# A two-layer decoder trunk on one core: the distance between weight splits kept between units of weights instead of between their parts

## The chip, the cores and the metric

The kernel runs on one core of one Trainium2 chip. The metric is the device time of one execution in microseconds (us). The core's engines are named as the profile names them: PE (TensorE, matmuls; PEld is its weight load), DVE (VectorE), ACT (ScalarE), POOL (GpSimd) and SP (SyncE, which issues most DMAs here). Each engine works through its own list of instructions in the written order and waits at an instruction until what that one needs is done.

## What is computed

A trunk of two layers over 512 tokens and 16 prepended meta tokens, in float32, width 1024. Each layer is half a SwiGLU feed-forward step, a token mixer, and another half feed-forward step, each with an RMSNorm on its input and its output. The mixer of the first layer is gated linear attention. The second layer, which the change touches, attends locally: 16 query heads, 4 shared key/value heads, blocks of 128 queries that see the block before, their own block up to themselves, and the 16 meta keys:

```python
q = (hn @ w_q).reshape(B, L, N_KV_HEADS, GROUP, HEAD_DIM)
q = (apply_partial_rope(q, cos, sin) * (HEAD_DIM ** -0.5)).transpose(0, 2, 3, 1, 4)
s = jnp.einsum('bkgnqd,bknsd->bkgnqs', q_blk, k_band)
p = sink_softmax(s, mask, sink_b[None, :, :, None, None, None])
o_real = jnp.einsum('bkgnqs,bknsd->bkgnqd', p.astype(v.dtype), v_band)
return o @ w_out
```

## The kernel before

**Weights.** Every weight matrix is cut into units in the order of use. A unit is mostly 128 x 1024 numbers and is read in two parts of 128 x 512 into `raw` buffers, of which there are 11. A part is then split for PE into two rounded halves, whose sum is the float32 weight: ACT writes the high half (line 237), and DVE subtracts it from the raw part to give the low half (line 238). The split parts lie in 32 slots; `slot(i)` lets a unit's part wait until a slot is free. A product with a split weight takes three matmuls for each of the eight 128-wide blocks of the inner dimension, and blocks 0 to 3 use the unit's first part, 4 to 7 its second.

**What sets the order.** The program is written by generators (`Flow`, `Job`) that run against a clock of the writer's own. The clock goes forward with each matmul that is written and has nothing to do with the chip. A generator that yields a number is taken up again when the clock has gone that far. So the instructions of loading, splitting, softmax and output are written between the matmuls where the clock calls for them, and this order is fixed in the program. Each engine keeps it.

**Local attention (`swa`, from about 1345 to 1500 us of the profiled span).** Eight query units u of 128 columns hold two heads each, 64 rows apiece. The first four are made by `x_first`, the others by `x_units` one after the other (PE tile `x`, 128 x 512, bank of PSUM). Line 1170 to 1173 rotate a product into `q`: a shuffle on DVE, a multiplication on DVE which also frees the bank, and two operations on POOL. For each u, `soft` writes four blocks of scores: two matmuls `sc`, one for each head, on the upper and on the lower 64 rows of PE; then on DVE, for each of the two, a masked minimum that reads the bank (line 1285, two rows of the trace), on ACT the exponential (line 1292); then sum, reciprocal and division (lines 1294 to 1308; for the second head, POOL divides). `core` transposes the result (`pt` and `pp` on PE), copies it (line 1327 on ACT, line 1328 on DVE), and makes the output `o`, which line 408 and 409 split into `so`. Last come the output products `y`. PSUM has eight banks here, all from one pool; a matmul that begins a new tile waits until the bank's last reader is done.

Splits of query units 5 to 7 and of the output weights (`swa_out`) run in this stretch. There `gap[0]` is 2.2 in place of 0: it is the smallest distance, in the writer's clock, between two splits. `turn[0]` holds the time of the last one. Elsewhere in the program `gap[0]` is 0 and the changed lines do nothing.

Of the kernel before, what the change touches and what calls it, by code (L numbers as in the profile page):

```python
# [127 lines left out]
def trunk_kernel(ctx: ExitStack, tc, a, out):  # L128
    nc = tc.nc
    pe, act, dve, pool, sp = nc.tensor, nc.scalar, nc.vector, nc.gpsimd, nc.sync  # L130
    flow = Flow()
# [50 lines left out]
    gap, turn = [0.0], [0.0]  # L182
# [42 lines left out]
    def slot(i):  # L225

        while live[0] + sum(n for j, n in owed.items() if j < i) >= limit[0]:
            yield room[0]
        live[0] += 1
        owed[i] -= 1  # L230

    def raw_tile(name):
        return rp.tile([P, 512], F32, tag="raw", name=name)

    def split_part(i, raw, m):
        w = pair_tile(f"w{i}_{len(loaded[i])}")
        act.activation(w[:, 0, :m], raw[:, :m], AF.Copy)  # L237
        newest[0] = hold(dve.tensor_tensor(w[:, 1, :m], raw[:, :m], w[:, 0, :m].bitcast(F32), op=ALU.subtract))  # L238
        loaded[i].append(w)

    def split_unit(i, raws, x):
        yield 2.2
        if x is not None:
            yield x.built[1]
        for raw, m in raws:
            if gap[0]:
                turn[0] = max(turn[0] + gap[0], flow.clock)
                yield turn[0] - flow.clock
            yield from slot(i)
            bound[0] = x and x.low  # L250
            split_part(i, raw, m)
            bound[0] = None
# [40 lines left out]
    def load_unit():  # L293
        i = len(loaded)
        asked[0] += costs[i]
        owed[i] = costs[i]
        if isinstance(units[i], list):
            g, u = units[i]
            chains[0] += 1
            raws = [raw_tile(f"raw{i}_{k}") for k in range(5)]  # L300
            for k, src, c in ((0, g, 0), (3, u, 0), (4, g, 0), (2, u, 1), (1, g, 1)):
                sp.dma_start(raws[k], src[:, c * 512 : (c + 1) * 512])
                dma_end[0] = max(dma_end[0], flow.clock) + 512 * 1.5e-3
            names = ("11", "12", "22", "s1", "s2", "s3", "s4")
            loaded.append(({k: [] for k in names}, {k: Job(None) for k in names}))
            gen = split_pair(i, raws)
        else:
            n = units[i].shape[-1]
            raws = []
            for c in range(0, n, 512):  # L310
                m = min(512, n - c)
                raws.append((raw_tile(f"raw{i}_{c}"), m))
                sp.dma_start(raws[-1][0][:, :m], units[i][:, c : c + m])
            dma_end[0] = max(dma_end[0], flow.clock) + n * 1.5e-3
            loaded.append([])
            gen = split_unit(i, raws, behind_x[0])
        split_jobs.append(flow.spawn(gen, dma_end[0] - flow.clock))
# [1073 lines left out]
    raws = [[raw_tile(f"raw{i}_{c}") for c in (0, 512)] for i in range(2)]  # L1391
# [151 lines left out]
```

## Time and profile before

| | us |
|---|---|
| median of 3 runs (1861.32 to 1862.3) | 1862.29 |
| the profiled execution | 1861.54 |
| its span, first to last instruction | 1859.8 |
| PE busy in the span | 1843.0 |
| DVE busy | 1360.3 |
| ACT busy | 1006.5 |
| POOL busy | 314.9 |

The profile is of one execution. A row of its timeline gives the start in us from the span's start, the length of the group, the engine, the line, output tile and inputs, the shape, and how many instructions were put together; in brackets stands the idle time ahead of it and what ended it. Matmuls overlap, so the time that one costs PE is the distance to the start of the next row, not its length. A float32 matmul, such as a score, has two instructions in the trace, so x4 means two scores.

### The profile page before, as it was taken

What the parts mean: (1) busy time and instruction counts of PE and PEld (TensorE: products, weight loads), DVE (VectorE), ACT (ScalarE), POOL (GpSimd) and SP (SyncE); (2) the same over time, 40 slices, a digit from 0 to 9 for tenths busy, and PEclk for the clock granted to TensorE, in tenths of its full rate; (3) what the DMA queues carried; (4) which work ended last, traced back from release to release, by engine and by line L of the source; (5) the groups of instructions that cost most, each with busy time, mean ns of one, the idle gap of its engine ahead of it and who ended that gap; (6) DMA issues with size and microseconds to landing.
All of it is one profiled execution on the core that took longest, in us unless ns stands there. A gap on an engine that the chain in (4) does not pass through costs nothing.

```text
span 1859.8 us, 36852 instructions
## 1 busy us (share of the span) xinstructions
PE 1843.0 (99%) x14146; PEld 1758.7 (95%) x14146; DVE 1360.3 (73%) x2703; ACT 1006.5 (54%) x2191; POOL 314.9 (17%) x370
## 2 busy tenths in 40 slices
PE   8999999999999999999999999999999999999998
PEld 8999999999999999999999898989977898989897
DVE  7884758777585887584888785858799589858484
ACT  7662636564465575362665563536556566626363
POOL 2101011320002310101033001111353231010101
PEclk9999999999999999999999999999999999999999
DMA  5655656312113255565642456666311215565561
GB/s 199 154 151 137 155 147 161 125 58 80 57 47 114 69 147 159 131 156 136 169 159 58 104 154 154 150 154 169 127 58 47 80 43 137 156 146 161 142 177 47
DMA packets 132530, 231.32 MB, mean 124 GB/s; under 512 B 14848, under 2 KB 26624, under 8 KB 132352
## 3 DMA queue, kind: packets, MB, share of 16 engines
q1 hardware_dynamic: 111328, 191.07, 32.6%
q0 software_dynamic: 20736, 37.76, 13.0%
q8 instruction: 111, 1.82, 0.4%
q14 instruction: 67, 0.55, 0.1%
q10 hardware_dynamic: 288, 0.13, 0.0%
HBM read 226.80 MB, written 2.10 MB: 123 GB/s over the span
## 4 chain that ended last, share of the span: by engine, by line
PE 89%; DVE 7%; ACT 3%; issue 1%; DMA 0%; POOL 0%; DVEq 0%; SPq 0%; ACTq 0%
PE y L165 29%; PE a L165 22%; PE x L165 16%; PE c L165 10%; PE d L165 5%; PE o L165 1%; PE e L165 1%; PE yt L165 1%; PE po L165 1%; DVE w L238 1%; ACT w L237 1%; PE sc L165 1%; DVE H L473 1%; PE ps L165 0%; PE pt L177 0%
## 5 line engine op out<-in xcount | busy, mean ns | idle before, releaser
L270 POOL DMA_DIRECT2D raw<-in_w_in x144 | 126.0, 953 | 970.1 <-DMA raw<-in_w_in 316.6
L165 PE MATMUL y<-hidl0f,w 128*128 128x256 f32 (+1 forms) x2112 | 260.4, 285 | 0.0
L238 DVE TENSOR_TENSOR w<-raw,w 128x512 fp32r<-128x512 f32 x376 | 241.2, 669 | 25.4 <-ACT w L237 23.5
L165 PEld LDWEIGHTS y<-hidl0f,w 128*128 128x128 f32 x2112 | 258.6, 188 | 0.2
L264 ACT ACTIVATE w_s<-raw 128x512 fp32r<-128x512 f32 x288 | 177.7, 625 | 116.4 <-DVE raw L280 69.5
L265 DVE TENSOR_TENSOR w_s<-raw,w_s 128x512 fp32r<-128x512 f32 x288 | 195.2, 689 | 55.3 <-ACT w_s L264 53.4
L165 PE MATMUL y<-hidl1f,w 128*128 128x512 f32 (+1 forms) x1200 | 233.2, 354 | 0.0
L165 PEld LDWEIGHTS y<-hidl1f,w 128*128 128x128 f32 x1200 | 195.1, 188 | 32.9 <-DVE w L238 0.3
L237 ACT ACTIVATE w<-raw 128x512 fp32r<-128x512 f32 x376 | 206.7, 587 | 34.2 <-PE y L165 28.0
L265 DVE TENSOR_TENSOR w<-raw,w 128x512 fp32r<-128x512 f32 x216 | 145.6, 688 | 51.9 <-ACT w L264 51.0
L264 ACT ACTIVATE w<-raw 128x512 fp32r<-128x512 f32 x216 | 130.4, 620 | 43.1 <-PE y L165 37.6
L165 PE MATMUL x<-x_l0m,w 128*128 128x272 f32 (+1 forms) x1152 | 148.2, 287 | 0.0
L165 PEld LDWEIGHTS x<-x_l0m,w 128*128 128x128 f32 x1152 | 142.5, 188 | 1.2 <-issue 0.4
L601 DVE TENSOR_TENSOR Y<-y,Y 128x256 f32<-128x256 f32 (+2 forms) x160 | 75.5, 479 | 88.4 <-PE y L165 88.2
L165 PE MATMUL a<-zl0f_t,w_s 128*128 128x264 f32 x864 | 117.5, 285 | 0.0
L165 PE MATMUL a<-zl1f_t,w_s 128*128 128x256 f32 x864 | 114.5, 282 | 0.6 <-ACT c L892 0.4
L165 PEld LDWEIGHTS a<-zl0f_t,w_s 128*128 128x128 f32 x864 | 110.4, 188 | 0.0
L165 PEld LDWEIGHTS a<-zl1f_t,w_s 128*128 128x128 f32 x864 | 107.2, 188 | 1.7 <-ACT c L892 1.6
L403 POOL TENSOR_TENSOR acc_post<-acc_post,sq_post 128x256 f32<-128x256 f32 (+1 forms) x72 | 60.9, 847 | 263.5 <-ACT sq_post L402 260.7
L165 PE MATMUL x<-x_l0f,w 128*128 128x256 f32 (+1 forms) x768 | 97.7, 289 | 5.8 <-ACT w L237 5.6
L165 PEld LDWEIGHTS x<-x_l0f,w 128*128 128x128 f32 x768 | 96.0, 191 | 6.6 <-ACT w L237 5.6
L165 PE MATMUL x<-x_l1f,w 128*128 128x256 f32 (+1 forms) x576 | 92.2, 320 | 0.0
(394 smaller groups left out, 3371.3 us busy)
## 6 DMA issues: line engine op xcount, KB each, us to landing
raw<-in_w_in SPq DMA_DIRECT2D x424, 256.0 KB, 3.8
raw<-in_w_in POOLq DMA_DIRECT2D x144, 256.0 KB, 5.3
raw<-in_w_out SPq DMA_DIRECT2D x96, 256.0 KB, 3.5
raw<-in_w_last SPq DMA_DIRECT2D x48, 256.0 KB, 3.3
raw<-in_gla_in SPq DMA_DIRECT2D x48, 256.0 KB, 3.1
raw<-in_w_out SPq DMA_DIRECT2D x64, 128.0 KB, 3.0
raw<-in_gla_out SPq DMA_DIRECT2D x16, 256.0 KB, 2.7
raw<-in_w_q SPq DMA_DIRECT2D x16, 256.0 KB, 4.1
```

Of the source, the lines that this page charges most:

```text
L165: inst = pe.matmul(o, lhs, rhs, start=start, stop=stop, skip_group_check=onto)
L237: act.activation(w[:, 0, :m], raw[:, :m], AF.Copy)
L238: newest[0] = hold(dve.tensor_tensor(w[:, 1, :m], raw[:, :m], w[:, 0, :m].bitcast(F32), op=ALU.subtract))
L264: act.activation(w[:, 0, :512], src, AF.Copy)
L265: dve.tensor_tensor(w[:, 1, :512], src, w[:, 0, :512].bitcast(F32), op=ALU.subtract)
L270: pool.dma_start(dst, src, accum_op=ALU.add)
L403: pool.tensor_tensor(sums[0][:, :n], sums[0][:, :n], t[:, :n], op=ALU.add)
L473: dve.tensor_tensor(h, t, h, op=ALU.add)
L601: dve.tensor_tensor(y, p[:, :n], y, op=ALU.add)
```

## The change

Before, each of a unit's two parts takes the next turn, 2.2 of the writer's clock behind the one before. Two units that are waiting at the same time take turns alternately, so that their parts are written interleaved: the first part of unit 5, the first of unit 6, and so on. After, a unit takes one turn for both parts, 2 x 2.2 behind the turn before, and its second part is written right behind the first if a slot is free. No operation is added or removed; nothing about the work of an instruction changes.

```diff
-        for raw, m in raws:
-            if gap[0]:
-                turn[0] = max(turn[0] + gap[0], flow.clock)
+        for c, (raw, m) in enumerate(raws):
+            if gap[0] and c == 0:
+                turn[0] = max(turn[0] + gap[0] * len(raws), flow.clock)
                 yield turn[0] - flow.clock
             yield from slot(i)
```

Since the turns come otherwise, the matmuls between them come otherwise too. Three places are shown. In the names, `x_0_17190` or `x_0_17185` is the product of query unit 5, `w_0` and `w_1` are the first and second part of a unit's split weights, `sc_eb` is the score of head e in block b, and the last number counts buffers in the order of writing.

The first is on PE, at query unit 5, from its fourth block on; before:

```order
L165 MATMUL x_0_17190<-x_l1m_16674,w_0_17146 128x512 x3
L165 MATMUL x_0_17190<-x_l1m_16699,w_1_17187 128x512
L165 MATMUL sc_00_17213<-kz_12401,q_17037 128x144
L165 MATMUL sc_10_17215<-kz_12401,q_17037 128x144
L165 MATMUL sc_01_17230<-kz_12401,q_17037 128x272
L165 MATMUL x_0_17190<-x_l1m_16699,w_1_17187 128x512 x2
L165 MATMUL x_0_17190<-x_l1m_16719,w_1_17187 128x512 x3
L165 MATMUL x_0_17190<-x_l1m_16744,w_1_17187 128x512 x3
L165 MATMUL sc_11_17232<-kz_12401,q_17037 128x272
```

and after:

```order
L165 MATMUL x_0_17185<-x_l1m_16674,w_0_17146 128x512 x3
L165 MATMUL x_0_17185<-x_l1m_16699,w_1_17149 128x512 x3
L165 MATMUL x_0_17185<-x_l1m_16719,w_1_17149 128x512 x3
L165 MATMUL sc_00_17219<-kz_12401,q_17037 128x144
L165 MATMUL sc_10_17221<-kz_12401,q_17037 128x144
L165 MATMUL x_0_17185<-x_l1m_16744,w_1_17149 128x512 x3
L165 MATMUL x_0_17185<-x_l1m_16769,w_1_17149 128x512 x3
L165 MATMUL sc_01_17233<-kz_12401,q_17037 128x272
L165 MATMUL sc_11_17235<-kz_12401,q_17037 128x272
```

The scores of block 1 stood on the two sides of eight matmuls; now they are next to each other, and five more matmuls of the unit's second part stand ahead of the first score. On DVE, the second part's split `w_1_17187` stood 16 instructions behind that of the first, `w_0_17146`; now, as `w_1_17149`, it follows it directly.

The second is on DVE, at the product of query unit 6 (`x_0_17280`, after `x_0_17248`), which the rotation (lines 1170 and 1171) takes out of its bank; before:

```order
L1285 ISA s_0_17340,nm_17342<-sc_01_17367,away,nsink 128x272
L1285 ISA nm_17342 128x1
L1285 ISA s_1_17341,nm_17342<-sc_11_17369,away,nsink 128x272
L1285 ISA nm_17342 128x1
L238 TENSOR_TENSOR w_0_17373<-raw_0_17239,w_0_17373 128x512
L1170 STREAM_SHUFFLE sh_q_16_17384<-x_0_17280 128x512
L1171 TENSOR_TENSOR q_17383<-x_0_17280,csq 128x512
```

and after:

```order
L1170 STREAM_SHUFFLE sh_q_16_17376<-x_0_17248 128x512
L238 TENSOR_TENSOR w_0_17358<-raw_0_17175,w_0_17358 128x512
L238 TENSOR_TENSOR w_1_17361<-raw_512_17177,w_1_17361 128x512
L1171 TENSOR_TENSOR q_17375<-x_0_17248,csq 128x512
L1285 ISA s_0_17346,nm_17348<-sc_01_17387,away,nsink 128x272
L1285 ISA nm_17348 128x1
```

Two splits now stand between the two steps that empty the bank; the two minima of block 1, which stood ahead of these steps, come behind them.

The third is on DVE too, at the scores of the third query unit's last block (`sc_03` and `sc_13`) with the division of the second unit (lines 1305 and 1308) between them; before:

```order
L238 TENSOR_TENSOR w_1_17425<-raw_512_17174,w_1_17425 128x512
L1298 RECIPROCAL den_17260<-den_17260 128x8
L1285 ISA s_0_17340,nm_17342<-sc_03_17430,away,nsink 128x272
L1285 ISA nm_17342 128x1
L1305 TENSOR_TENSOR mt_17262<-Y,den_17260 128x16
L1305 TENSOR_TENSOR mt_17262<-Y,den_17260 128x48
L1308 TENSOR_TENSOR Y<-Y,den_17260 128x144
L1308 TENSOR_TENSOR Y<-Y,den_17260 128x816
L1305 TENSOR_TENSOR mt_17262<-Y,den_17260 128x16
L1305 TENSOR_TENSOR mt_17262<-Y,den_17260 128x48
L1285 ISA s_1_17341,nm_17342<-sc_13_17432,away,nsink 128x272
```

and after:

```order
L1298 RECIPROCAL den_17270<-den_17270 128x8
L238 TENSOR_TENSOR w_0_17431<-raw_0_17239,w_0_17431 128x512
L1305 TENSOR_TENSOR mt_17272<-Y,den_17270 128x16
L1305 TENSOR_TENSOR mt_17272<-Y,den_17270 128x48
L1308 TENSOR_TENSOR Y<-Y,den_17270 128x144
L1308 TENSOR_TENSOR Y<-Y,den_17270 128x816
L1305 TENSOR_TENSOR mt_17272<-Y,den_17270 128x16
L1305 TENSOR_TENSOR mt_17272<-Y,den_17270 128x48
L238 TENSOR_TENSOR w_1_17434<-raw_512_17241,w_1_17434 128x512
L1285 ISA s_1_17347,nm_17348<-sc_13_17441,away,nsink 128x272
```

The minimum of `sc_13`, whose bank PE's first `o` takes next, now has two splits ahead of it in this place where it had one.

The order differs only from query unit 5 to the last split of the output weights; behind that, each engine's list is as before. SP's list of loads has the same loads in the same order, and POOL's differs at one place, where a rotation and a division change places.

## The prediction

> **What bounds the kernel.** I read the page first: the busy times, then the chain that ended last.
>
> ```profile
> span 1859.8 us, 36852 instructions
> PE 1843.0 (99%) x14146; PEld 1758.7 (95%) x14146; DVE 1360.3 (73%) x2703; ACT 1006.5 (54%) x2191; POOL 314.9 (17%) x370
> ...
> PE 89%; DVE 7%; ACT 3%; issue 1%; DMA 0%; POOL 0%; DVEq 0%; SPq 0%; ACTq 0%
> ```
>
> PE is the bound, and DMA has no share of the chain. The change issues no matmul more or less, so it can only alter how long PE stands still or runs badly in the stretch whose order it changes. The table of stretches for it, from the first moved matmul on (length, then busy times of PE, PEld, DVE, ACT, POOL):
>
> ```profile
> 1377.40:1399.70 22.30, 20.05 (x100) 12.29 (x99) 22.13 (x73) 14.71 (x51) 13.97 (x13) 1.00 0.35 100
> 1399.70:1429.30 29.60, 29.41 (x287) 22.25 (x286) 27.29 (x92) 19.64 (x61) 10.29 (x10) 1.00 0.17 51
> 1429.30:1480.00 50.70, 50.70 (x406) 40.45 (x405) 33.40 (x104) 30.93 (x86) 7.73 (x8) 1.00 0.15 45
> ```
>
> DVE is full in the first stretch (22.13 of 22.30 us), nearly full in the second, and has room in the third. So up to about 1429 us PE and DVE run side by side at their limits, and it matters in which order DVE frees PE's banks. The waits of PE in the whole attention (1340 to 1515 us) are few:
>
> ```profile
> PE x L165 <- DVE w L238: 1.5, 1, 1.5
> PE sc L165 <- DVE q L1171: 0.7, 1, 0.7
> PE st_post_l1f L165 <- POOL acc_post L403: 0.3, 1, 0.3
> PE pt L177 <- DVE pt L1328: 0.2, 1, 0.2
> ```
>
> That is 2.7 us, of which the last but one lies behind the change. PE's timeline shows that this isn't all, for a second loss hides inside busy rows:
>
> ```profile
> 1377.42 0.97 PE L165 MATMUL sc<-kz,q 64*128 64x144 f32 x6
> 1379.90 2.13 PE L165 MATMUL x<-x_l1m,w 128*128 128x512 f32 x8 [1.51 <-DVE w L238]
> 1381.97 0.72 PE L165 MATMUL sc<-kz,q 64*128 64x272 f32 x2
> 1382.62 0.96 PE L165 MATMUL x<-x_l1m,w 128*128 128x512 f32 x3
> ...
> 1385.76 1.33 PE L165 MATMUL sc<-kz,q 64*128 64x272 f32 x4
> 1387.02 1.66 PE L165 MATMUL x<-x_l1m,w 128*128 128x512 f32 x6
> 1388.61 0.73 PE L165 MATMUL sc<-kz,q 64*128 64x272 f32 x4
> 1389.27 1.66 PE L165 MATMUL x<-x_l1m,w 128*128 128x512 f32 x6
> ...
> 1397.27 1.28 PE L165 MATMUL sc<-kz,q 64*128 64x272 f32 x6
> 1399.25 0.51 PE L165 MATMUL sc<-kz,q 64*128 64x144 f32 x2 [0.69 <-DVE q L1171]
> 1399.69 0.96 PE L165 MATMUL x<-x_l1m,w 128*128 128x512 f32 x3
> ...
> 1402.51 0.72 PE L165 MATMUL sc<-kz,q 64*128 64x272 f32 x2
> 1403.16 1.66 PE L165 MATMUL x<-x_l1m,w 128*128 128x512 f32 x6
> 1404.75 0.43 PE L165 MATMUL o<-pt,vt 128*64 128x128 f32 x2
> ...
> 1419.49 1.21 PE L165 MATMUL sc<-kz,q 64*128 64x272 f32 x4
> 1420.63 0.66 PE L177 MATMUL pt<-ident,s 128*128 128x128 f32 x4
> ```
>
> The two scores of a block, one for each head, cost 0.66 us together (1388.61 to 1389.27). One alone costs 0.65 (1381.97 to 1382.62, 1402.51 to 1403.16). So the heads run at the same time where they are written next to each other and both banks are free. A pair that is torn apart, by matmuls between them or by a bank that comes late, costs 0.65 more. At 1385.76 the pair stands together and still takes 1.26 to the next row, at 1419.49 it takes 1.14.
>
> **The change, part by part.** DVE's rows give the prices:
>
> ```profile
> 1371.18 1.05 DVE L238 TENSOR_TENSOR w<-raw,w 128x512 fp32r<-128x512 f32 x1
> 1378.93 2.05 DVE L238 TENSOR_TENSOR w<-raw,w 128x512 fp32r<-128x512 f32 x2
> ...
> 1389.79 0.68 DVE L238 TENSOR_TENSOR w<-raw,w 128x512 fp32r<-128x512 f32 x1
> ...
> 1398.53 0.66 DVE L1171 TENSOR_TENSOR q<-x,csq 128x512 f32<-128x512 f32 x1
> ...
> 1402.59 1.22 DVE L1308 TENSOR_TENSOR Y<-Y,den 128x144 f32<-128x144 f32 x2
> ...
> 1403.93 0.50 DVE L1285 CUSTOM_DVE_ANT_0 s<-sc,away,nsink 128x272 f32<-128x272 f32 x1
> 1404.35 0.08 DVE L1285 DVE_READ_ACCUMULATOR2_ANT nm<- 128x1 f32 x1
> ```
>
> A split costs DVE 0.68 alone and some 1.03 (2.05 / 2) where POOL works beside it; a minimum costs 0.42 (1403.93 to 1404.35).
>
> *The old wait goes: -1.5.* At 1379.90 PE waits for the second part of query unit 5, whose split DVE reaches at 1378.93 at the earliest. In the new order it follows the first part's, which starts at 1371.18, so it ends by about 1373.3, four microseconds ahead of PE's need. ACT's high half has to come forward as well: ACT stands idle for 3.56 us ahead of its next work at 1370.39 there, by the timeline, and takes it. That row and the later three splits:
>
> ```profile
> 1370.39 0.48 ACT L379 ACTIVATE R_l1m<-st_l1m,eps 128x256 f32<-128x256 f32 x1 [3.56 <-PE st_l1m L165]
> ...
> 1371.28 1.66 ACT L237 ACTIVATE w<-raw 128x512 fp32r<-128x512 f32 x3
> ```
>
> *Two pairs are joined: -1.3.* The order puts the scores of block 1 of the first and of the fourth unit side by side, which are the four lone scores at 1377.42 (last of its row) and 1381.97, and ahead of and at 1402.51. Two times 0.65.
>
> *A third pair gets its banks in time: -0.6.* At 1385.76 the second score takes the bank that a minimum of block 2 frees. Ahead of that, DVE takes the product of unit 5 out of its bank, and PE's wait had made that product late: its last matmuls stand at 1382.62 and end at 1383.6. In the new order they end three microseconds earlier, so DVE gets through to the minimum about 1 us sooner, and PE finds the bank free. 1.26 - 0.66.
>
> *A wait that stays, a little longer: +0.6.* The block of scores at 1397.27 takes 2.42 us to 1399.69 in place of the 0.9 that a 272 pair and a 144 pair need (0.55 and 0.35, the first without the 0.1 for the change back to `x`), since its banks come from the rotation (1398.53) and from the minima behind it. In the new order PE arrives with 2.7 us of lead (the first three terms, less what the joins gave at 1402), while the rotation has two splits between its steps but two minima fewer ahead. I place its end at 1397.1 to 1398.4; the last bank is free after three more minima, 1.3 later. PE, there at about 1396.0 (1397.27, six more matmuls of 0.23, less 2.7), leaves at 1398.6 to 1399.9. The loss was 1.5 and is 1.7 to 2.9: +0.2 to +1.4. I take +0.6, nearer to the low end, as DVE starts the stretch with less waiting behind POOL.
>
> *A new wait: +0.7.* The first `o`, at 1404.75, needs the bank that the minimum ending at 1404.43 frees. This had 0.3 to spare. PE now comes at about 1403.8 (its lead of 2.1, and five more matmuls, 1.16, done ahead). DVE has one split more ahead of that minimum, 0.6, and had gained 0 to 1.2 by then: release at 1403.8 to 1405.0, a wait of 0 to 1.2; the middle is taken.
>
> *Later: -0.5 and +0.4.* The pair at 1419.49 waited for the last rotation and a copy; both come earlier in the new order (1.14 - 0.66). The second `o` needs a copy on DVE which stands behind the last block's minima; PE comes to it over 2 us earlier than before, and I allow 0.4 (0 to 1.2, by the wait of the first `o`).
>
> *Nothing:* the loads. SP waits for raw buffers, and those are given back with the split:
>
> ```profile
> 1368.46 33.87 SPq L313 DMA_DIRECT2D raw<-in_swa_out  x13
> ```
>
> They are all issued by 1402.3, stay in order, and none waits for a split that the change makes later by more than 0.6 us; the one whose split is moved forward most, by about 4 us at 1408, has been issued over 20 us before. POOL's exchanged rotation and division end two microseconds before PE needs either. Were this cover gone, it would cost as long as a POOL row, 1.7 us.
>
> Sum: -1.5 - 1.3 - 0.6 + 0.6 + 0.7 - 0.5 + 0.4 = **-2.2 us**. Its bounds, by the ends of the terms: -5.4 if the two waits come out at zero and the loss at 1397.27 goes too (-1.5 - 1.3 - 0.6 - 1.5 - 0.5), and +0.2 with every new wait at its upper end (-1.5 - 1.3 - 0.6 + 1.4 + 1.2 - 0.5 + 1.2, rounded up by 0.3 for PE's idle edges). The profiled execution took 1861.54 and would take 1859.3; it stands 0.75 below the median of the runs, which makes **1860.1** against 1862.29.
>
> [...] DVE and POOL slow each other here:
>
> ```profile
> 1380.40 1.74 POOL L1172 TENSOR_TENSOR sh_q<-sh_q,csq 128x512 f32<-128x512 f32 x1
> ...
> 1398.70 1.27 POOL L1172 TENSOR_TENSOR sh_q<-sh_q,csq 128x512 f32<-128x512 f32 x1 [1.28 <-DVE sh_q L1170]
> ```
>
> The same POOL operation takes 1.74 us beside two splits and 1.27 at 1398.70; the splits lose 0.35 each. [...] This trace shows 0.35 a split, so I stay with the rows.
>
> **Rivals.** *DVE sets the pace and nothing is gained (within 0.5 us of before).* For it: DVE is busy for 22.13 of 22.30 us and its work is the same, so PE's lead can be taken back whole at the first `o`. Against: by then PE has five more `x` matmuls behind it, and these 1.16 us aren't lost again. Time 1862.1.
>
> *All releases come in time.* If DVE, with fewer meetings with POOL, runs 1.2 us ahead of my estimate, the waits at 1397 and 1404 don't appear: -5.0, 1857.3. For it: two waits of the sum are worked out, not seen. Against: it needs both, and PE is early at both.
>
> *Slower: pairs of splits tear pairs of scores.* Two splits in a row hold DVE for 1.2 to 2.05 us in which no bank is freed, and PE comes to the banks earlier than before. Of 32 pairs (8 units, 4 blocks), each newly torn one costs 0.65. Against the firm gains of 3.4 the change turns slower from the sixth on, and by over 0.2% (3.7 us) from the eleventh: 1866.0. For it: two pairs (1385.76, 1419.49) are torn by late banks already. Against: five torn pairs are all that the timeline has now, and DVE's total is unchanged.
>
> **How the numbers follow.** 0.2% is 3.7 us, about what a measurement of this kernel can tell from no change. The forecast has 0.56 (its own range 1858.6 to 1862.2), no gain 0.10; both are within 0.2%, together 0.66. All in time has 0.22 and is faster. Torn pairs have 0.12 and are slower. The range from 1857.4 to 1864.0 leaves out about 0.08 below and 0.11 above.
>
> **What would show it.** In the profile after: no wait of PE `x` for DVE `w` near 1379; the waits of PE for DVE `q`, and for a minimum (`nm`) at the first `o`, near 1397 and 1403; pairs of 272-wide scores at 0.66 to the next row near 1381 and 1400; the first `y` with `so` at 1427 in place of 1429.3; behind that, the same lengths as before. It would be wrong if PE kept its lead there and lost it up to 1480, or if DVE's splits in pairs took over 1.1 us each.

## The result

The change makes the kernel slower by 3.15 us: 1865.43 us (median of 22 runs, 1864.01 to 1866.94) against 1862.28 (22 runs, 1861.32 to 1865.5). The ratio is 1.0014, its 95% interval 1.0008 to 1.002. That lies within the 0.2% to which the forecast gave 0.66, but on the other side of zero, above the range (1857.4 to 1864.0), and near the time of the rival that was slower.

The page after, with the chain's shares:

```profile
span 1862.6 us, 36852 instructions
PE 1843.3 (99%) x14146; PEld 1760.5 (95%) x14146; DVE 1363.6 (73%) x2703; ACT 1006.1 (54%) x2191; POOL 316.6 (17%) x370
...
PE 88%; DVE 8%; ACT 2%; issue 1%; POOL 0%; DMA 0%; DVEq 0%; SPq 0%; ACTq 0%; POOLq 0%
```

The span is 2.8 us longer, and DVE has 8% of the chain in place of 7%. PE's waits from 1340 to 1515 us, after:

```profile
PE sc L165 <- DVE q L1171: 3.7, 1, 3.7
PE sc L165 <- DVE so L409: 1.3, 1, 1.3
PE st_post_l1f L165 <- POOL acc_post L403: 0.2, 1, 0.2
PE sc L165 <- DVE nm L1285: 0.2, 1, 0.2
```

The wait of 1.5 for `w` is gone, as forecast. The one for `q` went from 0.7 to 3.7, and a wait of 1.3 for `so` is new. PE's timeline after, at the places of the forecast:

```profile
1380.80 0.73 PE L165 MATMUL sc<-kz,q 64*128 64x272 f32 x4
1381.46 1.65 PE L165 MATMUL x<-x_l1m,w 128*128 128x512 f32 x6
...
1384.83 1.18 PE L165 MATMUL sc<-kz,q 64*128 64x272 f32 x6
1386.20 0.72 PE L165 MATMUL sc<-kz,q 64*128 64x272 f32 x2 [0.19 <-DVE nm L1285]
...
1400.84 2.17 PE L165 MATMUL sc<-kz,q 64*128 64x272 f32 x8 [3.69 <-DVE q L1171]
1402.94 1.65 PE L165 MATMUL x<-x_l1m,w 128*128 128x512 f32 x3
1404.39 0.65 PE L177 MATMUL pt<-ident,Y 128*128 128x128 f32 x4
...
1405.29 0.73 PE L165 MATMUL sc<-kz,q 64*128 64x272 f32 x4
1405.95 0.50 PE L165 MATMUL x<-x_l1m,w 128*128 128x512 f32 x1
...
1422.05 1.32 PE L165 MATMUL sc<-kz,q 64*128 64x272 f32 x4 [1.26 <-DVE so L409]
...
1431.91 0.95 PE L165 MATMUL y<-so,w 128*128 128x512 f32 x3
```

The first and the second joined pair cost 0.66 each (1380.80 to 1381.46, 1405.29 to 1405.95). The third pair stays torn. Counting PE's work matmul by matmul (an `x` matmul more or less as 0.23), the changed kernel leads by 1.6 us at 1397. It lags by 2.5 at 1405, ahead of the second joined pair, by 1.6 at the first `o`, by 1.2 at the second, and by 2.6 from 1424 on. The first `y` comes at 1431.91 in place of 1429.30, and behind it the distance stays. So the loss has two places: 4.1 us at the rotation near 1400, of which the joined pair gives 0.9 back, and 1.4 near 1421.

The first place holds two losses. One is the wait. The other comes behind it, where three `x` matmuls take 1.65 in place of the usual 0.96. The table of stretches (length, busy PE, PEld, DVE, ACT, POOL, then the granted clock):

```profile
1400.00:1402.00 2.00, 1.16 (x5) 1.06 (x6) 2.00 (x9) 0.76 (x3) 1.07 (x1) 0.77 0.53 167
1402.00:1404.00 2.00, 2.00 (x9) 1.53 (x7) 2.00 (x10) 2.00 (x6) 0.20 (x1) 0.50 0.15 55
1404.00:1406.00 2.00, 2.00 (x14) 1.27 (x12) 2.00 (x8) 1.40 (x6) 0.25 (x1) 0.88 0.30 93
```

The clock that PE is granted falls to 0.50 behind the wait; in quarter-microsecond stretches it is down from 1401.06 to 1404.47, which is 3.41 us. In the kernel before it is 1.00 all through this part.

Why is `q` late? DVE after, first two rows where POOL is idle, then the way to the rotation, then the way to `so`:

```profile
1390.28 0.16 DVE L1294 TENSOR_TENSOR es<-nm,vec 128x8 f32<-128x8 f32 x1
1390.36 1.28 DVE L238 TENSOR_TENSOR w<-raw,w 128x512 fp32r<-128x512 f32 x2
...
1395.81 1.49 DVE L1294 TENSOR_TENSOR es<-nm,vec 128x8 f32<-128x8 f32 x1
1397.23 0.72 DVE L1170 STREAM_SHUFFLE sh_q<-x 128x512 f32<-128x512 f32 x1
1397.85 2.34 DVE L238 TENSOR_TENSOR w<-raw,w 128x512 fp32r<-128x512 f32 x2
1400.11 0.68 DVE L1171 TENSOR_TENSOR q<-x,csq 128x512 f32<-128x512 f32 x1
...
1417.88 0.89 DVE L1297 TENSOR_TENSOR den<-den,es 128x8 f32<-128x8 f32 x1
...
1419.05 1.20 DVE L1305 TENSOR_TENSOR mt<-s,den 128x16 f32<-128x16 f32 x2
```

and POOL after:

```profile
1395.34 1.93 POOL L1308 TENSOR_TENSOR Y<-Y,den 128x144 f32<-128x144 f32 x2 [6.11 <-ACT Y L1292]
1398.03 1.61 POOL L1172 TENSOR_TENSOR sh_q<-sh_q,csq 128x512 f32<-128x512 f32 x1 [0.75 <-DVE sh_q L1170]
...
1417.47 1.28 POOL L1172 TENSOR_TENSOR sh_q<-sh_q,csq 128x512 f32<-128x512 f32 x1 [0.76 <-DVE sh_q L1170]
1418.83 1.27 POOL L1173 TENSOR_TENSOR q<-q,sh_q 128x512 f32<-128x512 f32 x1
```

The addition `es`, of eight numbers in each row, takes 0.16 alone and 1.49 here, and ends (when the shuffle starts, 1397.23) with POOL's division (1395.34 + 1.93 = 1397.27). The pair of splits takes 1.28 alone and 2.34 beside POOL's product. Near 1418 `den` (0.89, to 1418.77) and `mt` (1.20, to 1420.25) wait out the last rotation's two POOL operations, one each (to 1418.75 and 1420.10). DVE's operations that read PSUM, such as the shuffle and the minima, keep their lengths: in this trace a 512-wide shuffle takes 0.74 beside POOL at 1382.46 and 0.72 at 1397.23, where POOL rests, and a 272-wide minimum 0.50 beside POOL at 1383.51 and 0.49 at 1391.56, where it rests.

### The profile page after: what moved, and what is told of

The parts are those of the page before. It is cut to its first block, busy times and chain, and to the rows that moved or that the text cites. A ratio compares the mean times of both kernels' runs of the same rounds, so it can differ in the third digit from the quotient of the medians.

```text
span 1862.6 us, 36852 instructions
## 1 busy us (share of the span) xinstructions
PE 1843.3 (99%) x14146; PEld 1760.5 (95%) x14146; DVE 1363.6 (73%) x2703; ACT 1006.1 (54%) x2191; POOL 316.6 (17%) x370
## 4 chain that ended last, share of the span: by engine, by line
PE 88%; DVE 8%; ACT 2%; issue 1%; POOL 0%; DMA 0%; DVEq 0%; SPq 0%; ACTq 0%; POOLq 0%
PE y L165 29%; PE a L165 22%; PE x L165 15%; PE c L165 10%; PE d L165 5%; DVE w L238 1%; PE e L165 1%; PE yt L165 1%; PE o L165 1%; PE po L165 1%; ACT w L237 1%; DVE H L473 0%; PE sc L165 0%; PE ps L165 0%; DVE Y L1285 0%
```

## Two theories

*The meeting with POOL:* a DVE operation with both inputs in SBUF, as `es` above (0.16 and 1.49) or the pair of splits (1.28 and 2.34), stands still while a POOL instruction runs, and in the new order more of these stand just ahead of the two releases that PE waits for. *The place alone:* it costs that two splits stand between shuffle and product, whatever POOL does. A third, raised with the run of the late pair: PE's banks are late from further up.

The tables in the next sections give the profiled span, and the median less that of the kernel before in the same comparison, with the ratio and its 95% interval.

## Experiments: POOL's work left out

Both kernels lose POOL's divisions and its 512-wide rotation steps, in one run each; its 256-wide steps, which end at 1384, stay. Then the changed kernel loses only a part of this. In none of them does an instruction of PE, DVE or ACT change its place.

```diff
-        pool.tensor_tensor(sh, sh, s, op=ALU.mult)
-        pool.tensor_tensor(dst, dst, sh, op=ALU.add)
+        if n != 512:
+            pool.tensor_tensor(sh, sh, s, op=ALU.mult)
+            pool.tensor_tensor(dst, dst, sh, op=ALU.add)
...
-                        (pool if e else dve).tensor_tensor(tt, tt, dv.to_broadcast([P, n, w]), op=ALU.mult)
+                        if not e:
+                            dve.tensor_tensor(tt, tt, dv.to_broadcast([P, n, w]), op=ALU.mult)
```

The run without divisions has the last three lines alone. The run without one product leaves out the first of the two rotation lines where `name` is `"q6_16"`, the rotation at 1398.

> The changed kernel without POOL's work in this stretch: the divisions of the second heads (L1308) and both 512-wide steps of the last rotations (L1172, L1173) are left out, every other engine's instructions and their order stay. Theory one, the meeting with POOL: DVE's operations with two operands in SBUF stand still while a POOL instruction runs, so es falls from 1.49 to 0.16 us and the pair of splits behind the shuffle from 2.34 to 1.28; the bank is free 2.4 earlier or more, PE's wait for q falls from 3.7 to at most 1.3, the wait for so at 1422 (1.3) goes, and the span falls from 1862.6 to 1857.0 to 1858.5. Theory two, the place alone: what costs is that two splits stand between the shuffle and the product, whatever POOL does; the wait falls by less than 0.5 and the span stays above 1861.5.

> The kernel before with the same POOL work left out. Theory one: the before loses less to POOL, since fewer of its two-operand operations stood beside it just ahead of a release that PE waited for: span 1858.0 to 1859.0 (1859.8 less the wait of 0.7 for q and up to 1.1 at the torn pairs), the old wait for w near 1379 stays at 1.0 to 1.5. Then the changed kernel without POOL is the faster of the two, by 0.5 to 2.5 us, as the prediction had it for the change. Theory two: the changed one stays slower, by 1 to 2.8 us.

> The changed kernel with only the divisions on POOL (L1308 of the second heads) left out, the rotations kept, all orders the same. Theory one: es 0.16 instead of 1.49, the pair of splits still near 2.3 since it meets the rotation's product; PE's wait for q falls by 1.3 to about 2.4, span 1861.0 to 1861.5. Theory two: wait 3.7, span 1862.6.

> The changed kernel with one POOL instruction left out: the 512-wide product (L1172) of the rotation at 1398, which ran beside the pair of splits; all orders stay. Theory one, the meeting with POOL: the pair falls from 2.34 to 1.28 us, es keeps its 1.49 (it met the division, which stays); PE's wait for q falls by 1.06 to 2.6, the granted clock still goes to 0.5 for some 3.4 us behind it as in the changed kernel and in the one without divisions, span 1861.3 to 1861.8. Theory two, the place alone: wait 3.7, span 1862.6.

| | span | median to before | ratio |
|---|---|---|---|
| after, no POOL work | 1856.5 | -4.64 | 0.9974 (0.9964 to 0.9983) |
| before, no POOL work | 1857.5 | -2.96 | 0.9985 (0.9976 to 0.9994) |
| after, no divisions | 1860.5 | +0.51 | 1.0002 (0.9993 to 1.0011) |
| after, one product less | 1862.3 | +1.90 | 1.0008 (0.9998 to 1.0017) |

After without POOL's work, DVE's way to the rotation and the waits of PE:

```profile
1394.87 0.16 DVE L1296 TENSOR_TENSOR es<-nm,vec 128x8 f32<-128x8 f32 x1
1394.95 0.73 DVE L1170 STREAM_SHUFFLE sh_q<-x 128x512 f32<-128x512 f32 x1
1395.58 1.28 DVE L238 TENSOR_TENSOR w<-raw,w 128x512 fp32r<-128x512 f32 x2
```

```profile
PE sc L165 <- DVE q L1171: 0.4, 1, 0.4
PE o L165 <- DVE nm L1287: 0.4, 1, 0.4
```

Before without it:

```profile
PE x L165 <- DVE w L238: 1.5, 1, 1.5
```

Without that work the two splits still stand between shuffle and product, and PE waits 0.4. PE comes to the block at the same time in both (1397.14 and 1397.15), and its wait is 3.3 shorter: 1.33 at `es`, 1.06 at the pair, and 0.94 by which DVE reaches `es` earlier (1394.87 against 1395.81). This third part is made further up, where the splits near 1385 and 1387 take 0.68 and 0.69 in place of 1.20 and 1.61. The changed kernel is then the faster one, by 1.0 us of span and 1.7 of the medians (4.64 - 2.96), near what the prediction had thought the change to be worth (2.2); its slowest run, 1858.55, is faster than the fastest run of the kernel before, 1858.76. So the place alone falls. By the medians, the POOL work left out costs the kernel before 3.0 us and the changed one 7.8 (3.15 + 4.64); what waits for POOL's results is in that too, and what meets it.

The parts add up too. Without the divisions, and without the one product:

```profile
1396.09 0.16 DVE L1294 TENSOR_TENSOR es<-nm,vec 128x8 f32<-128x8 f32 x1
...
1396.81 2.35 DVE L238 TENSOR_TENSOR w<-raw,w 128x512 fp32r<-128x512 f32 x2
```

```profile
1396.58 1.49 DVE L1295 TENSOR_TENSOR es<-nm,vec 128x8 f32<-128x8 f32 x1
...
1398.62 1.27 DVE L238 TENSOR_TENSOR w<-raw,w 128x512 fp32r<-128x512 f32 x2
```

Each takes away its own operation's stop and leaves the other's. The waits for `q` are 2.4 and 2.6, 1.3 and 1.1 below the changed kernel's 3.7; both were forecast. By the medians the two gain 2.6 and 1.25 us on the changed kernel. The spans were not as good: the first three in the table lie 0.5 below their ranges, and the last one, 1862.3, lies 0.5 above its own, since its profiled execution reaches 1396 later by 0.8 from far ahead of the change. Without the divisions the wait for `so` falls to 0.3 as well.

## Experiments: the work moved

*The pair later.* The turn of one unit of weights comes 1.0 of the writer's clock later, so that its pair stands behind the product and the next two minima.

```diff
-                yield turn[0] - flow.clock
+                yield turn[0] - flow.clock + (1.0 if i == 213 else 0.0)
```

> The changed kernel with one unit of weights later by 1.0 us of the planner's clock, so that its two splits stand behind the product of the rotation and the next two minima instead of between shuffle and product; nothing is left out. Both theories: PE's wait for q falls by the pair's 2.3, to about 1.4. Theory one says that the gain is 2.3 (1.28 of work and 1.06 of standing still), so the span falls to about 1860.5 (1860.0 to 1861.5, since the splits now hold up the later minima a little); a third theory, that PE's banks are late from further up, leaves the wait above 2.5 and the span above 1862.

Span 1864.1, +3.13, ratio 1.002 (1.0011 to 1.0029): no gain, a clear miss of the forecast. The wait for `q` is the 1.4 that was forecast, but the pair, 2.36 us long beside POOL, now stands ahead of the next minima, and PE waits there:

```profile
PE sc L165 <- DVE nm L1285: 2.4, 2, 2.2
PE sc L165 <- DVE q L1171: 1.4, 1, 1.4
```

```profile
1400.10:1406.80 6.70, 4.70 (x14) 3.34 (x14) 6.70 (x21) 3.00 (x8) 1.85 (x3) 0.50 0.55 155
```

The clock is at 0.50 through the whole 6.70 us of this row, in which DVE is busy throughout. The pair that meets POOL is late here for the minima behind it, at the price of PE's wait of 2.2. The third theory isn't borne out as the whole cause: `q` came as early as the pair's move allows, and by the run without POOL's work 0.94 of the wait is made further up.

*Other ways to keep part of the change.* Units of weights 2.2 apart with their parts together; the first unit's parts alone together; the same with one split later and, on ACT, the division of the first query unit's second head; and a unit's turn of 4.4 with its parts 2.2 apart. The first and the last are edits of the changed kernel, the other two of the kernel before.

```diff
-                turn[0] = max(turn[0] + gap[0] * len(raws), flow.clock)
+                turn[0] = max(turn[0] + gap[0], flow.clock)
```

```diff
-        for raw, m in raws:
-            if gap[0]:
+        joined = gap[0] and turn[0] == 0.0
+        for raw, m in raws:
+            if gap[0] and not (joined and raw is not raws[0][0]):
```

```diff
+                        if e and u == 0:
+                            for q in range(n):
+                                act.activation(tt[:, q], tt[:, q], AF.Identity, scale=den[:, e, b + q : b + q + 1])
+                        else:
...
```

```diff
                 yield turn[0] - flow.clock
+            elif gap[0]:
+                yield gap[0]
```

> The two parts of a unit follow each other as in the change, but units stand 2.2 apart instead of 4.4; so no split stands between shuffle and product of the rotation near 1397, and four splits follow each other near 1379. If adjacency as such costs, span 1862 or more. By theory one the cost is where the splits meet POOL and a release that PE waits for: es still meets the division (1.3 lost), the rotation ends near 1398.4, PE waits 0.8 to 1.6 for q there, which leaves the granted clock at 1.00, and the four splits near 1379 beside POOL's 256-wide rotations tear one to three pairs of scores (0.65 each): span 1858.5 to 1860.8.

> The kernel before, with the parts of the first unit alone following each other (the one whose second part PE waited for at 1379), the other parts taking turns as before. The place alone, read from the prediction's firm terms: the old wait of 1.5 goes, one pair is joined (0.65), one split stands between shuffle and product, 0.7: span 1858.0 to 1858.8. By theory one that split stands beside POOL's product and es beside its division (1.0 and 1.4 instead of 0.68 and 0.39): the rotation ends 2.0 later than without POOL, PE waits 1.5 to 2.5 for q, and where the wait is above 2 the clock falls to 0.5: span 1859.3 to 1862.0.

> As the last, with two things more: the second head's division of the first attention unit is done by ACT (four activations, 1.9 us by ACT's rows of 0.40 and 0.51) instead of POOL, and one split comes 1.0 us of the planner's clock later, so that nothing stands between shuffle and product. Theory one: es takes 0.16, the product ends 2.0 to 2.4 earlier than with that split and the division on POOL, PE's wait for q is below 0.5, no drop of the clock: span 1857.5 to 1859.0, the fastest of all that compute everything. If ACT's 1.9 us delay an exponential or a copy that PE waits for, the span is 1860 or more and the wait shows as one of PE for ACT.

> The change's turn for a unit (4.4 in place of 2.2 a part) is kept, its other half undone: the second part comes 2.2 after the first instead of right behind it. If parts that follow each other are what costs, the waits are near those of before: q 0.5 to 1.5, no drop of the clock, span 1859.0 to 1860.8. If units that stand 4.4 apart are what costs, span 1862 or more with a wait for q above 2.

| | span | median to before | ratio |
|---|---|---|---|
| units 2.2 apart | 1863.2 | +3.71 | 1.0020 (1.0011 to 1.0029) |
| first unit alone | 1864.3 | +4.08 | 1.0025 (1.0014 to 1.0035) |
| the same, division on ACT | 1862.9 | +2.08 | 1.0013 (1.0003 to 1.0022) |
| parts apart | 1862.9 | +2.54 | 1.0013 (1.0004 to 1.0023) |

All four spans lie above their ranges, so my sums for a new order were too good here as well. What I had costed at the rotation came about: with the first unit alone `es` takes 1.48 and PE waits 2.0 for `q`; with the division on ACT `es` takes 0.16 and no wait for `q` is left, but PE waits 0.5 for a copy on ACT. But each order has other meetings that my sums did not have. Three of the four wait 1.1 to 1.2 for `so`, near 1421 as the change does. With the first unit's parts together three splits follow each other at 1380, beside POOL's rotations, and take 3.77 us; with units 2.2 apart four take 5.43, and PE waits 1.9 for a minimum behind them and 1.6 for copies on ACT. Each half of the change alone costs about as much as both (3.71 and 2.54 against 3.15), by waits of its own. So neither the adjacency of the parts nor the distance of the units is the cause by itself.

*The pair earlier, without and with the division on ACT; the kernel before with the division on ACT.* The first has `-1.0` in place of `1.0` in the edit of the late pair. The other two have the edit for ACT above, which leaves PE's and DVE's order as it is.

> The changed kernel with the unit whose splits stood between shuffle and product 1.0 us of the planner's clock earlier: its pair then stands at about 1392, where POOL is idle. The meeting with POOL: the pair costs 1.28 instead of 2.34, es still meets the division (1.0 to 1.5); PE's wait for q falls from 3.7 to 1.9 to 2.6, which still takes the granted clock to 0.5 for 3.4 us; span 1861.0 to 1862.0. If the place between shuffle and product were the whole cause, the wait would fall by the pair's 2.3 to 1.4 and the span to 1859.5 to 1860.5.

> The last kernel, and the second head's division of the first unit on ACT besides; PE and DVE keep the last kernel's order. The meeting with POOL: es falls to 0.16, the wait for q to 0.6 to 1.2, the clock stays at 1.00, so the gain over the last is the wait's 1.3 and the half clock's 1.4: span 1858.5 to 1860.0. If POOL were not the cause, it is as the last.

> The kernel before, with one thing changed: the second head's division of the first attention unit (the POOL row of 2.36 us at 1395.06) is done by ACT in four activations; the order of PE and DVE stays as it was. By the meeting with POOL, es falls from 0.39 to 0.16 us and the split at 1396.70 from 1.27 to 0.68, so the rotation ends 0.8 earlier, PE's wait of 0.7 for q goes and one torn pair at 1397 with it: span 1858.3 to 1859.2 against 1859.8, faster by 0.6 to 1.5. If ACT's four activations (1.9 us, ahead of es and of the next exponentials) delay what PE waits for: 1859.8 or more.

| | span | median to before | ratio |
|---|---|---|---|
| pair earlier | 1862.3 | +1.56 | 1.0008 (0.9999 to 1.0017) |
| pair earlier, division on ACT | 1861.1 | +0.29 | 1.0000 (0.9991 to 1.0009) |
| before, division on ACT | 1860.9 | -1.00 | 0.9994 (0.9986 to 1.0003) |

Where the pair meets no POOL, near 1394, its splits take 0.68 and 0.63; `es` still takes 1.48 and PE waits 1.8. With the division on ACT the wait is 0.5, and 1.27 us of the medians are gained by where one division is done; 2.7 had been forecast. The spans again are above the ranges, in part by the clock, which fell for 3.41 us in both kernels with the division on ACT, at 1420 and at 1380.5. The last kernel also has a wait of 0.4 for a copy on ACT and one of 0.4 for a minimum; its median is below that of the kernel before by 1.00, within the forecast 0.6 to 1.5, but its interval reaches past 1.

*The last rotation on DVE.* What stayed open was the second place, near 1421: division or rotation.

```diff
+        if name == "q7_16":
+            hold(dve.tensor_tensor(sh, sh, s, op=ALU.mult))
+            hold(dve.tensor_tensor(dst, dst, sh, op=ALU.add))
+            return
         pool.tensor_tensor(sh, sh, s, op=ALU.mult)
```

> The changed kernel with product and sum of the last rotation (L1172, L1173 at 1417 to 1420) done by DVE instead of POOL; PE's order stays, DVE has two operations more (0.68 each), and so and the copy behind it come ahead of the division. If the meeting with the rotation is the rest of the second loss: den 0.16 instead of 0.89, mt 0.29 instead of 1.20, the wait for so at 1422 is gone or below 0.3, the first wait stays at 3.7: span 1861.0 to 1861.8, median 1.0 to 1.6 below the changed kernel's. If the division alone were it: the wait for so stays near 1, span 1862.6 or more, since DVE has 1.3 us more to do.

Span 1861.6, +2.22, ratio 1.0010 (1.0001 to 1.0019). The waits:

```profile
PE sc L165 <- DVE q L1171: 3.7, 1, 3.7
PE st_post_l1f L165 <- POOL acc_post L403: 0.3, 1, 0.3
```

The wait for `so` is gone and the other untouched; `den` takes 0.16. DVE does 1.3 us more and PE gains 1.0, or 0.9 by the medians (3.15 - 2.22), just under the forecast 1.0 to 1.6; in this profile the clock is down for 6.83 us near 1400, in place of 3.41. One thing is mixed in: `so` also came ahead of the division on DVE, so this run shows that the rotation's part can be had back, not how much of it is the meeting.

*Both places cleared, all work done.* Pair earlier, last rotation on DVE, and the second heads' divisions of one unit (`u == 0`) or of three (`u < 3`) on ACT.

> The early pair and the first unit's division on ACT, and the last rotation on DVE as in the kernel above: no POOL operation beside the work ahead of either release. The meeting with POOL: wait for q 0.5, for so below 0.3, the wait for a minimum (0.8) stays; span 1859.0 to 1860.0, at or a little below the kernel before (ratio 0.998 to 1.000). If order and not POOL were the cause, it is like the changed kernel, 1862 or more.

> The same with the second heads' divisions of the first three units on ACT (twelve activations, 5.7 us by ACT's rows) instead of one unit's. The meeting with POOL: es at 1407 and 1416 falls from 0.9 and 0.75 to 0.16, which helps the minimum that PE waits 0.8 for at the first o only if it stands behind; span 1858.3 to 1859.6. If ACT's additional work delays an exponential or a copy that PE waits for, 1860 or more, with a wait of PE for ACT.

With one unit's division moved: span 1859.0, -1.29, ratio 0.9992 (0.9983 to 1.0001). With three: span 1858.0, 1860.30 us against 1862.24, -1.94, ratio 0.9986 (0.9977 to 0.9995), faster than both kernels. Its waits:

```profile
PE pt L177 <- DVE nm L1289: 0.8, 2, 0.4
PE o L165 <- DVE nm L1289: 0.8, 1, 0.8
PE sc L165 <- DVE q L1171: 0.5, 1, 0.5
```

These are 2.1 us, and with two more of 0.2 each 2.5 in all, where the changed kernel's four waits above sum to 5.4. The wait at the first `o` that the prediction had put at 0.7 is there with 0.8, now that PE comes early enough to meet it.

## Why the prediction was wrong

- *The old wait goes, -1.5:* right.
- *Two pairs are joined, -1.3:* right; a joined pair costs 0.66.
- *A third pair gets its banks in time, -0.6:* wrong. The two splits ahead of it take 1.20 and 1.61 beside POOL's rotations, and PE waits 0.19. PE's lead at 1397 was 1.6 and not 2.7.
- *A wait that stays, a little longer, +0.6 (+0.2 to +1.4):* this is the step that failed. The term was the loss at the block of scores, 1.5 before. After, the wait is 3.69, and the block and three `x` matmuls behind it take 3.55 (1400.84 to 1404.39). At full clock and with a wait of 0.5 they take 2.50, as the kernel with the earlier pair and the division on ACT shows (without POOL's work, 2.49):

```profile
1398.10 1.77 PE L165 MATMUL sc<-kz,q 64*128 64x272 f32 x8 [0.51 <-DVE q L1171]
1399.80 0.96 PE L165 MATMUL x<-x_l1m,w 128*128 128x512 f32 x3
1400.60 0.60 PE L177 MATMUL pt<-ident,Y 128*128 128x128 f32 x4
```

  Of those 3.55 some 0.9 + 0.8 are the work itself, so the loss is 3.69 + 1.85 = 5.5, and the term +4.0 in place of +0.6. By the runs above, the loss of 5.5 has 2.4 from the two meetings (1.33 at `es`, 1.06 at the pair), 0.94 from meetings further up, and 1.05 (3.55 - 2.50) from the half clock; some 1.2 are left without POOL's work. My end of the rotation, 1397.1 to 1398.4, stands 2.3 us ahead of the real 1400.7. The text doesn't work it out; by its prices a split lost 0.35 beside POOL, and `es` isn't named. One sign of being wrong was named there, splits in pairs of over 1.1 us each, and it came: 1.17 each for the pair of 2.34.
- *A new wait at the first `o`, +0.7:* did not come, because PE was late by then.
- *Later, -0.5 and +0.4:* +1.4 and 0. The last rotation came earlier, as I wrote, and for that reason its POOL operations fell on `den` and `mt`, ahead of `so`.
- *The price of a meeting with POOL:* here the choice was wrong. The row gave 0.35 a split as a mean over two splits, and such a mean doesn't tell how long each of them stood still; I took it as the price of any meeting, and an addition of eight numbers a row then lost 1.33 at one. The kernel before had shown as much, in rows that the prediction does not have:

```profile
1400.57 0.80 DVE L1297 TENSOR_TENSOR den<-den,es 128x8 f32<-128x8 f32 x1
...
1404.92 1.00 DVE L1294 TENSOR_TENSOR es<-nm,vec 128x8 f32<-128x8 f32 x1
```

```profile
1400.05 1.29 POOL L1173 TENSOR_TENSOR q<-q,sh_q 128x512 f32<-128x512 f32 x1
1403.97 1.93 POOL L1308 TENSOR_TENSOR Y<-Y,den 128x144 f32<-128x144 f32 x2 [2.63 <-DVE mt L1305]
```

  Alone such an operation takes 0.16. DVE's next rows start at 1401.29 and 1405.85, and POOL's rows end at 1401.34 and 1405.90. In the changed kernel `es` at 1395.81 ends with POOL's division to within 0.04 us (1397.23 and 1397.27). With the lengths measured since, 1.33 at `es` and 1.06 at the pair ahead of the rotation, the meetings add 2.4 to the +0.6.
- *The rivals:* *DVE sets the pace* had the right engine, since PE's lead was taken back at DVE's releases, but it held DVE's work to be the same, and DVE's busy time grew from 1360.3 to 1363.6 us. Pairs of scores torn by pairs of splits was the slower one, and at 1866.0 it gave nearly the time by luck, since the way was another: no pair was torn that had not been before. That POOL could stop DVE just ahead of a release had no chance of its own. The half clock was nowhere in it.

## What to carry over

Where an order on DVE changes, look at what runs on POOL at the moment of each release that the critical engine waits for, and cost each operation by the whole POOL instruction that it may meet, not by a mean slowdown: the mean was 0.35 a split, and `es` lost 1.33. Small operations counted here as much as large ones: an addition of eight numbers a row, 0.16 us alone, held a bank for 1.3 us more. And a wait on PE can be dearer than its length: behind the one of 3.69 us the clock was at 0.50 for 3.41, which cost 1.05 more.

## What was not expected of the hardware

The clock's steps. In the profiles of nine of the fifteen runs, with a mean granted clock of 0.997 or 0.998, and of the changed kernel (0.998) it fell. In quarter-microsecond stretches it is down to 0.50 for 3.41 us in the changed kernel, with the pair earlier, with that and the division on ACT, and in the kernel before with the division on ACT, and for 6.83 with the last rotation on DVE. How little idle time it takes is not a matter of the wait alone. PE's wait of 1.5 for `w` is there in the kernel before and in the one with the division on ACT. The stretch behind it, in the kernel before and in the other:

```profile
1380.60:1383.90 3.30, 3.30 (x16) 1.95 (x16) 3.13 (x12) 1.66 (x7) 3.22 (x3) 1.00 0.55 163
```

```profile
1380.60:1383.90 3.30, 3.30 (x9) 2.14 (x7) 2.58 (x8) 1.59 (x7) 3.22 (x3) 0.50 0.55 167
```

The same wait, and once the clock stayed and once it halved (9 matmul instructions in place of 16). Nor does PE's busy time ahead of the fall tell them apart: in the second kernel PE was busy for 1.88 of the 3.41 us ahead of it (1377.11 to 1380.52), with the earlier pair and the division on ACT for 2.07 (1416.77 to 1420.18), while the kernel before kept the full clock through a stretch with 1.90 of 3.41 (1376.50 to 1379.91). Nor is there a length of wait that decides it: I had expected a fall above a wait of 2, an estimate between the 1.5 of the kernel before, with no fall, and the 3.7 of the changed one, and it fell behind the 1.5 of the second row. What decides it stays open. The fall also makes one profiled span uncertain. The kernel before ran 33 times beside the early pair: the 27 runs with a mean granted clock of 0.999 took 1861.8 us on average, the six with 0.998 took 1864.5. That the clock alone makes this difference is not shown. All 22 runs of the changed kernel have 0.997 or 0.998. So the verdicts above go by the medians.
